# Forgetting attention in a two-layer trunk: values' products 12 steps later, V in two buffers, bias transfers on SyncE's queue, split last weight parts

## The chip, the cores and the metric

The kernel runs on one core of one Trainium2 chip. The core has five engines with an instruction stream each: TensorE (PE, matrix products into the accumulators of PSUM), VectorE (DVE), ScalarE (ACT), GpSimd (POOL) and SyncE (SP, which here only asks for transfers). The metric is the device time of one execution in microseconds, and lower is better.

## What is computed

Two decoder layers on one sequence of 256 tokens, model width 2048, in float32. Layer 0 mixes tokens with forgetting attention, 32 heads of 64; layer 1 with sliding-window attention. Cut to layer 0, which is all that the change touches:

```python
h = rmsnorm(x, norm_g[0])
p = h @ fox_w_in[0]                      # 2048 x 8224: q, k, v, gate, and 32 columns for log_f
q, k, v, gate = ...
log_f = log_sigmoid(p[..., 4*W:] + fox_b_f[0])
c = cumsum(log_f, axis=1)
s = (q @ k.T) * 64**-0.5 + c[t] - c[s]   # per head; masked where key > query
y = softmax(s) @ v
x = x + (y * silu(gate)) @ fox_w_out[0]
```

Layer 1 has the same frame with other attention, and a final RMSNorm ends the trunk.

## The kernel before, in words

**Products.** Each float32 product is made of split operands. A part of a weight matrix arrives as `wraw` by a DMA of SP's queue (`load`, L211, or L207 where one part is made of two blocks); ACT copies its leading bits into the "high" half of `w` (CAST, L224) and DVE subtracts to get the "low" half (L225). The activations lie in `xs` (layer input) or `ys` (attention output) as high and low too. Of a unit of weights (256 output columns, all 2048 inputs, four parts of four 128-row tiles), each tile gives two "wide" matmuls (512 columns: weight high by activation high and low) and two "narrow" ones (256 columns: weight low by activation high). The values' units run the other way round, activations as the stationary operand and three 512-column matmuls a tile. All matmuls have one line, L83, since a helper issues them; they are told apart by their tiles. There are five buffers for `w` and four for `wraw`, two accumulators `acc` for units and one more, `ps_s`, for scores; a third unit of the output projection borrows it.

**Stages of layer 0.** The 32 heads are eight groups of four (g = 0 to 7). A group has units q, k, gate, and values; the values of groups 1 and 2, 3 and 4, 5 and 6 come as one unit. Behind the last group comes the output projection (`out_units`), eight units whose results are added into `xT`. When a unit's last matmul is done, its consumer runs: for k, DVE adds the two halves (L613), scales (L614), ACT and DVE split the result in `kk` (L618, L619, L621, L622). For an output unit, ACT copies the upper half out (L319) and DVE adds twice (L736, L737), which sets the accumulator free for the unit three places on.

**Attention of a pair of heads.** It has stages, each on its own: the bias c[s] of the pair's keys is spread over 128 partitions by a DMA from `negc_d` into `bc` (L665, issued by POOL) and masked by POOL (L127); the scores of the second query block (`s`, PE from `kk` and `q` into `ps_s`, DVE L432 and L413); the scores of the first block some steps later (`s_first`); the softmax (ACT L361, DVE L369, L372); a transposition in two moves: DVE L453 into `staged`, a DMA to `turned_d` (L458) and four DMAs back into `pts` (L463), all issued by POOL; the values' products (PE `psy` from `pts` and `vg`), the gate (L547), and the split of the result into `ys` (L554).

**The order.** The matmuls stand in the program's order. The weight parts form one stream, and attention is hung into it: `tick` counts a step for every second matmul (every one and a half in the values' units), and a stage is registered to come so many steps after its group's k has been consumed. These numbers are tables, FOX_DUE for even groups, FOX_ODD, FOX_FIRST (group 0), FOX_NEXT (group 1) and FOX_LAST (group 7): for each of the two pairs of heads of a group the step of the first scores and the distance to the second ones, and then the step of the values' products. A bias is asked for 14 steps ahead of its scores (BIAS), or as many as the table's third number says. The other engines' order and SP's are set by a scheduler from dependencies and priorities: the consumers and the stages of attention have a raised one. Which transfers SP asks for and when follows from buffers: a weight part waits until the DVE instruction that read the buffer before it is done.

## Time and profile before

| what | us |
|---|---|
| three runs | 807.16, 811.65 (median), 812.43 |
| the profiled execution | 806.58 |
| span of its program | 804.8 |
| PE busy | 791.6 |
| DVE busy | 646.9 |
| ACT busy | 516.5 |
| POOL busy | 116.3 |

Of the span, layer 0's groups take about the first 403 us, its output projection what follows up to about 490 us. The granted TensorE clock was 0.997 of full speed. A row of the timeline reads: start, duration, engine, line, operation, output tile from input tiles, shapes, count, and in brackets how long the engine had been idle and what ended that. A row of the waits reads: engine, tile and line that waited, what it waited for, microseconds in all, times, the longest. "SPq" and "POOLq" are the queues of transfers that these engines ask for.

### The profile page before, as it was taken

How to read it: one execution, taken by the hardware profiler on the slowest of the kernel's cores; microseconds unless marked ns; L12 is line 12 of the kernel's file. 1: busy time of each engine (PE TensorE's matmuls, PEld its weight loads, DVE VectorE, ACT ScalarE, POOL GpSimd, SP SyncE). 2: the span in 40 equal slices, each digit the busy share in tenths (PEclk: the TensorE clock that was granted, in tenths of full speed). 3: DMA queues.
4: the chain of work that ended last, by engine and by line, in shares of the span. 5: the costliest groups of instructions: out<-in, count | busy, mean ns of one | idle time of the engine just before them, and what ended most of it. 6: DMA issues, size and time to landing. Idle time of an engine off the chain costs nothing.

```text
span 804.8 us, 13739 instructions
## 1 busy us (share of the span) xinstructions
PE 791.6 (98%) x4994; PEld 695.0 (86%) x4994; DVE 646.9 (80%) x1148; ACT 516.5 (64%) x947; POOL 116.3 (14%) x182
## 2 busy tenths in 40 slices
PE   8999999999999999999999999999999999999996
PEld 7988788888888888888888888888888888888885
DVE  6998986898688886888848768668999999977654
ACT  6876665665556565566537556567788786875651
POOL 1012340133202222021113110200000000001210
PEclk9999999999999999999999999999999999999998
DMA  8757797587866877577665655856445554455632
GB/s 276 253 195 267 243 302 214 177 269 234 249 186 202 257 252 240 189 214 247 195 218 170 210 188 161 223 155 209 153 158 189 185 180 152 155 192 188 198 122 105
DMA packets 52596, 164.43 MB, mean 204 GB/s; under 512 B 6977, under 2 KB 10209, under 8 KB 52529
## 3 DMA queue, kind: packets, MB, share of 16 engines
q1 hardware_dynamic: 44640, 141.84, 55.4%
q0 software_dynamic: 6736, 20.26, 9.0%
q10 hardware_dynamic: 1152, 1.47, 0.5%
q8 instruction: 39, 0.64, 0.3%
q14 instruction: 29, 0.23, 0.1%
HBM read 154.84 MB, written 8.70 MB: 203 GB/s over the span
## 4 chain that ended last, share of the span: by engine, by line
PE 84%; DVE 7%; DMA 4%; ACT 2%; issue 2%; SPq 0%; POOL 0%; DVEq 0%; ACTq 0%
PE acc L83 79%; DMA wraw<-in_fox_in_dram 3%; PE ps_s L83 2%; PE psy L83 2%; DVE w L225 2%; DMA pts<-turned_d 1%; ACT st L361 1%; DMA turned_d<-staged 1%; DVE st L372 1%; DVE staged L453 1%; DVE st L413 1%; DVE kk L622 1%; DVE kk L621 1%; PE psy_s L83 0%; ACT w L224 0%
## 5 line engine op out<-in xcount | busy, mean ns | idle before, releaser
L83 PE MATMUL acc<-xs,w 128*128 128x256 f32 (+1 forms) x2624 | 468.2, 337 | 0.3 <-ACT w L224 0.3
L83 PEld LDWEIGHTS acc<-xs,w 128*128 128x128 f32 x2624 | 404.6, 190 | 53.7 <-issue 0.7
L225 DVE TENSOR_TENSOR w<-wraw,w 128x1024 fp32r<-128x1024 f32 (+4 forms) x277 | 322.7, 1179 | 87.6 <-ACT w L224 86.6
L224 ACT CAST w<-wraw 128x1024 fp32r<-128x1024 f32 (+4 forms) x277 | 274.3, 1010 | 167.9 <-PE acc L83 122.1
L83 PE MATMUL acc<-ys,w 128*128 128x256 f32 (+1 forms) x960 | 168.3, 337 | 0.0
L83 PEld LDWEIGHTS acc<-ys,w 128*128 128x128 f32 x960 | 147.7, 190 | 19.4 <-issue 0.5
L83 PE MATMUL acc<-w,xs 128*128 128x512 f32 (+2 forms) x512 | 108.3, 361 | 1.1 <-ACT w L224 1.1
L83 PEld LDWEIGHTS acc<-w,xs 128*128 128x128 f32 x512 | 86.9, 188 | 16.1 <-ACT w L224 1.6
L361 ACT ACTIVATE st<-st,mx 128x256 f32<-128x256 f32 (+1 forms) x128 | 56.5, 443 | 12.6 <-DVE mx L413 8.1
L319 ACT COPY half<-acc 128x512 f32<-128x512 f32 x56 | 32.6, 583 | 33.1 <-PE acc L83 32.8
L463 POOL DMA_DIRECT2D pts<-turned_d x64 | 35.2, 556 | 55.5 <-DMA turned_d<-staged 40.2
L757 POOL TENSOR_TENSOR acc<-acc,sq 128x256 f32<-128x256 f32 x28 | 26.7, 954 | 82.5 <-ACT sq L751 81.4
L755 POOL COPY acc<-sq 128x256 f32<-128x256 f32 x2 | 1.3, 637 | 239.3 <-ACT sq L751 239.3
L83 PE MATMUL ps_s<-kk,q 128*128 128x256 f32 (+1 forms) x160 | 31.1, 307 | 2.0 <-DVE kk L622 1.4
L127 POOL TENSOR_SCALAR_AFFINE_SELECT bc<-bc 128x256 f32<-128x256 f32 x32 | 22.5, 720 | 70.4 <-DMA bc<-negc_d 70.4
L83 PEld LDWEIGHTS ps_s<-kk,q 128*128 128x128 f32 x160 | 24.8, 190 | 6.1 <-issue 3.0
L665 POOL DMA_DIRECT2D bc<-negc_d x16 | 9.0, 560 | 115.2 <-issue 101.6
L361 ACT ACTIVATION_READ_ACCUMULATOR st<-st,mx 128x1 f32 x128 | 24.0, 187 | 0.0
L380 ACT ACTIVATE st<-st,rl 128x128 f32<-128x128 f32 x64 | 23.9, 445 | 0.1
L159 DVE SCALAR_TENSOR_TENSOR xs<-xT,g_sb,xs 128x256 fp32r<-128x256 f32 x32 | 20.4, 667 | 3.5 <-ACT xs L158 3.5
L413 DVE CUSTOM_DVE_ANT_0 st<-ps_s,st 128x256 f32<-128x256 f32 (+1 forms) x64 | 20.3, 350 | 0.5
L158 ACT ACTIVATE xs<-xT,g_sb 128x256 fp32r<-128x256 f32 x32 | 15.5, 501 | 8.1 <-DVE xT L737 7.4
(144 smaller groups left out, 579.8 us busy)
## 6 DMA issues: line engine op xcount, KB each, us to landing
wraw<-in_fox_in_dram SPq DMA_DIRECT2D x96, 512.0 KB, 4.9
wraw<-in_swa_in_dram SPq DMA_DIRECT2D x72, 512.0 KB, 4.3
wraw<-in_fox_out_dram SPq DMA_DIRECT2D x32, 512.0 KB, 4.7
wraw<-in_swa_out_dram SPq DMA_DIRECT2D x32, 512.0 KB, 4.4
wraw<-in_fox_in_dram SPq DMA_DIRECT2D x54, 256.0 KB, 4.9
bc<-negc_d POOLq DMA_DIRECT2D x16, 384.0 KB, 5.2
turned_d<-staged POOLq DMA_DIRECT2D x16, 384.0 KB, 4.8
pts<-turned_d POOLq DMA_DIRECT2D x64, 96.0 KB, 5.3
```

The lines of the kernel that those rows point to most:

```text
L83: tc.keep_in_program_order(nc.tensor.matmul(*args, **kw))
L127: return nc.gpsimd.affine_select(out=ap, in_=ap, compare_op=ALU.is_ge, fill=NEG, base=base, pattern=pattern, channel_multiplier=mult,)
L158: nc.scalar.activation(xs[:, kt, 0, :], xT[:, kt, :], AF.Copy, scale=g)
L159: nc.vector.scalar_tensor_tensor(out=xs[:, kt, 1, :], in0=xT[:, kt, :], scalar=g, in1=xs[:, kt, 0, :].bitcast(F32), op0=ALU.mult, op1=ALU. ...
L224: state["split"] = nc.scalar.copy(high, raw)
L225: state["lows"] = [*state.get("lows", [])[-1:], nc.vector.tensor_tensor(out=low, in0=raw, in1=high.bitcast(F32), op=ALU.subtract)]
L319: nc.scalar.copy(s, ps[:, :, S : 2 * S])
L361: nc.scalar.activation(st[:, hh, rng], st[:, hh, rng], AF.Exp, scale=sign, bias=nm[:, qb, hh : hh + 1], accum_out=l[:, qb, hh : hh + 1],)
L380: nc.scalar.mul(st[:, hh, rng], st[:, hh, rng], rl[:, qb, hh : hh + 1])
L413: nc.vector.tensor_tensor_reduce(out=st, in0=high, in1=st if low is None else low, scale=self.scale, scalar=self.start(hh), op0=ALU.add, o ...
L463: nc.gpsimd.dma_start(out=pts[b * B : (b + 1) * B], in_=turned_d[b].rearrange("(a j) x -> j a x", j=B))
L757: nc.gpsimd.tensor_add(sums[0], sums[0], s)
```

## The change

- The values' products come 12 steps later in FOX_DUE and FOX_LAST, 15 in FOX_FIRST; those of FOX_NEXT and FOX_ODD keep their number.
- First scores move: the odd groups' from 22 to 27 and from 51 to 56, group 1's from 28 to 32 and from 59 to 64, the even groups' from 21 to 22 and from 52 to 50; group 1's second scores come 15 steps after the first instead of 12. Group 7's scores stay.
- The biases are asked for by SP instead of POOL, and 20 to 40 steps ahead of the scores instead of 14.
- `vg` (V) has two buffers instead of one. To make room, q and k share one tile, and a tile `r08` (the norm's scale times 1/8) is gone: q is scaled by one SCALAR_TENSOR_TENSOR instead of a TENSOR_TENSOR. Group 0's staging tiles are renamed to fit.
- The last of the four parts of the first three units of layer 0's output projection is two parts of two tiles each, and unit 0's last addition is put ahead of the two latest low subtractions on DVE.

```diff
--- before.py
+++ after.py
@@ -38,11 +38,11 @@
 SCALE_DUE = 8
 
 
-FOX_DUE = ((21, 12), (52, 13), 138)
-FOX_LAST = ((24, 12), (48, 13), 122)
-FOX_ODD = ((22, 12), (51, 12), 118)
-FOX_FIRST = ((57, 16, 32), (81, 12), 170)
-FOX_NEXT = ((28, 12), (59, 14), 120)
+FOX_DUE = ((22, 12, 20), (50, 13, 30), 150)
+FOX_LAST = ((24, 12, 20), (48, 13, 30), 134)
+FOX_ODD = ((27, 13, 25), (56, 13, 35), 118)
+FOX_FIRST = ((57, 16, 32), (81, 12, 40), 185)
+FOX_NEXT = ((32, 15, 25), (64, 14, 40), 120)
 SWA_DUE = ((36, 65), (53, 81), 91)
 SWA_LAST = ((36, 63), (51, 78), 86)
 
@@ -604,12 +604,14 @@
             with tc.high_priority(HP):
                 t = fox.tile([P, 2, S], F32, tag="q", name="q", bufs=1)
                 nc.vector.tensor_add(t, ps[:, :, 0:S], low_half(ps))
-                nc.vector.tensor_mul(t, t, each(state["r08"][:, 0:S]))
+                nc.vector.scalar_tensor_tensor(
+                    out=t, in0=t, scalar=SCALE, in1=each(r0()[:, 0:S]), op0=ALU.mult, op1=ALU.mult
+                )
                 self.qT = stack_q(t)
 
         def k(self, ps):
             with tc.high_priority(HP):
-                t = fox.tile([P, 2, S], F32, tag="k", name="k", bufs=1)
+                t = fox.tile([P, 2, S], F32, tag="q", name="k", bufs=1)
                 nc.vector.tensor_add(t, ps[:, :, 0:S], low_half(ps))
                 nc.vector.tensor_mul(t, t, each(r0()[:, 0:S]))
 
@@ -633,7 +635,7 @@
 
             def consume(c, ps):
                 if c == 0:
-                    self.vt = fox.tile([P, 2, 512], F32, tag="vg", name="vg", bufs=1)
+                    self.vt = fox.tile([P, 2, 512], F32, tag="vg", name="vg", bufs=2)
                     self.vg, other.vg = [None, None], [None, None]
                 nc.scalar.mul(self.vt[:, c, :], ps, r0()[:, S + c : S + c + 1])
                 self.vg[c], other.vg[c] = (self.vt[:, c, i * 256 : (i + 1) * 256] for i in range(2))
@@ -642,7 +644,7 @@
 
         def v(self, c, ps):
             if c == 0:
-                self.vt = fox.tile([P, 2, 512], F32, tag="vg", name="vg", bufs=1)
+                self.vt = fox.tile([P, 2, 512], F32, tag="vg", name="vg", bufs=2)
                 self.vg = [None, None]
             vg = self.vg[c] = self.vt[:, c, 0:256]
             if self.g > 0:
@@ -662,7 +664,7 @@
 
                 assert "forgot" in state
                 bc = fox.tile([P, 2, 3 * P], F32, tag="bc", name="bc")
-                nc.gpsimd.dma_start(out=bc, in_=negc_d[h0 : h0 + 2, :].partition_broadcast(P))
+                nc.sync.dma_start(out=bc, in_=negc_d[h0 : h0 + 2, :].partition_broadcast(P))
                 for hh in range(2):
                     diagonal = bc[:, hh, :].rearrange("p (b k) -> p b k", k=P)[:, 0:3:2, :]
                     filled = fill_where_not(diagonal, [[0, 2], [-1, P]], 0, 1)
@@ -705,10 +707,11 @@
             uq, uk = (
                 Unit(
                     cut(lambda a, b, w=fox_in_d[i, 0]: w[a // 8][:, a % 8 : a % 8 + b - a], QK_PARTS),
-                    "wgt", consume, stages=(half, (fox, own, 2 * S, 1), None, gt) + more, acc=acc,
+                    "wgt", consume, stages=(half, own, None, gt) + more, acc=acc,
                 )
                 for i, own, consume, more, acc in (
-                    (0, "q", G.q, (gt,), None), (1, "k", G.k, ((fox, "vg", 4 * S, 1),), (ps_s, "S")),
+                    (0, (fox, "q", 2 * S, 1), G.q, (gt,), None),
+                    (1, (fox, "pts_odd", 12 * P, 1), G.k, ((fox, "vg", 4 * S, 2),), (ps_s, "S")),
                 )
             )
             units += [uv, uq, uk, whole(fox_in_d[3, g], "wgt", gate_consumer(r0, G))]
@@ -734,16 +737,27 @@
             def consume(ps):
                 x = xT[:, 2 * u : 2 * u + 2, :]
                 nc.vector.tensor_add(x, low_half(ps), x)
-                nc.vector.tensor_add(x, ps[:, :, 0:S], x)
+                last = nc.vector.tensor_add(x, ps[:, :, 0:S], x)
+                if u == 0 and src is fox_out_d:
+                    ahead_of_lows(last)
                 for c in range(2):
                     done(2 * u + c)
 
             return consume
 
-        first = [
-            whole(src[u], "wgt", consumer(u), acts=ys, acc=(ps_s, "S") if u == 2 else None)
-            for u in range(3)
-        ]
+        def ends_late(u):
+            halves = [(src[u][1][:, k : k + 2, :], [2]) for k in (4, 6)]
+            return Unit(
+                quarters(src[u])[0:3] + halves, "wgt", consumer(u), acts=ys, acc=(ps_s, "S") if u == 2 else None
+            )
+
+        if src is fox_out_d:
+            first = [ends_late(u) for u in range(3)]
+        else:
+            first = [
+                whole(src[u], "wgt", consumer(u), acts=ys, acc=(ps_s, "S") if u == 2 else None)
+                for u in range(3)
+            ]
         return first + [whole(src[u], "wgt", consumer(u), acts=ys) for u in range(3, 8)]
 
     def square_into(sums, m):
@@ -1049,16 +1063,14 @@
         state["r0"] = r = inv_rms(
             [ssq0[:, 0, :]], "n0", ps_t.tile([P, 512], F32, tag="T", name="ps_n0")
         )
-        r08 = cpool.tile([P, S], F32, name="r08")
-        nc.vector.tensor_scalar_mul(r08, r[:, 0:S], SCALE)
-        state["r08"] = r08
 
     def in_turn(units):
         return [(u, p) for u in units for p in range(len(u.parts))]
 
     def out_stream(units):
 
-        early = [(u, p) for u in units[0:3] for p in range(3)] + [(u, 3) for u in units[0:3]]
+        late = len(units[0].parts) - 1
+        early = [(u, p) for u in units[0:3] for p in range(late)] + [(u, late) for u in units[0:3]]
         return early + in_turn(units[3:])
 
 
@@ -1123,7 +1135,9 @@
     def breaks(u, p):
 
         if u in turns:
-            return p in (1, 2) or p == 3 and u not in (first_out[0], last_out[0])
+            if u in first_out:
+                return p in (1, 3) or p == 4 and u is not first_out[1]
+            return p in (1, 2) or p == 3 and u is not last_out[0]
         return p % 2 == 1
 
     prev, held, wide_first = None, [], True
```

The number of matmuls and their sizes are the same. How instructions move is shown at three places.

PE, around the first pair's scores of group 5. Where `w` comes first in a row's inputs the matmuls are those of the values' unit of groups 5 and 6, `ps_s` are the scores (512 columns the first ones, 256 the second ones), `psy` the values' products of groups 3 and 4. Before, and with the change:

```order
L83 MATMUL acc<-xs,w 128x512 x14
L83 MATMUL acc<-xs,w 128x256 x32
L83 MATMUL acc<-xs,w 128x512 x16
L83 MATMUL acc<-w,xs 128x512 x33
L83 MATMUL ps_s<-kk,q_2702 128x512 x2
L83 MATMUL acc<-w,xs 128x512 x18
L83 MATMUL ps_s<-kk,q_2702 128x256 x2
L83 MATMUL acc<-w,xs 128x512 x12
L83 MATMUL psy<-pts,vg 64x256
```

```order
L83 MATMUL acc<-xs,w 128x512 x18
L83 MATMUL acc<-xs,w 128x256 x32
L83 MATMUL acc<-xs,w 128x512 x16
L83 MATMUL acc<-w,xs 128x512 x41
L83 MATMUL ps_s<-kk,q_2727 128x512 x2
L83 MATMUL acc<-w,xs 128x512 x19
L83 MATMUL ps_s<-kk,q_2727 128x256 x2
L83 MATMUL acc<-w,xs 128x512 x21
L83 MATMUL psy<-pts,vg 64x256
```

The first scores stand eight matmuls later, the second ones nine, and the values' products 18 later.

DVE, around the scaling of group 7's k (L614 before, L616 with the change). L453 writes `staged` of the pair before. Before, and with the change:

```order
L225 TENSOR_TENSOR w<-wraw,w 128x4x256
L453 STREAM_TRANSPOSE staged<-st 128x6x4x32
L613 TENSOR_TENSOR k<-acc,half 128x512
L225 TENSOR_TENSOR w<-wraw,w 128x4x256
L614 TENSOR_TENSOR k<-k,r_n_492 128x512
L621 TENSOR_TENSOR kk<-k,kk 64x2x256
L622 TENSOR_TENSOR kk<-k,kk 64x2x256
```

```order
L225 TENSOR_TENSOR w<-wraw,w 128x4x256
L453 STREAM_TRANSPOSE staged<-st 128x6x4x32
L225 TENSOR_TENSOR w<-wraw,w 128x4x256 x2
L615 TENSOR_TENSOR k<-acc,half 128x512
L616 TENSOR_TENSOR k<-k,r_n_492 128x512
L225 TENSOR_TENSOR w<-wraw,w 128x4x256
L623 TENSOR_TENSOR kk<-k,kk 64x2x256
```

The scaling of k now follows the addition at once; before, a low subtraction of a weight part (L225) stood between them. One more L225 stands ahead of the addition.

PE, at the end of the output projection's first three units. `acc` of the highest number here belongs to unit 3, which takes over the accumulator of unit 0, `acc_4064` before and `acc_4062` with the change. Before, and with the change:

```order
L83 MATMUL acc_4192<-ys_81,w_4155 128x512 x8
L83 MATMUL acc_4064<-ys_81,w_4168 128x512 x8
L83 MATMUL acc_4128<-ys_81,w_4189 128x512 x8
L83 MATMUL acc_4064<-ys_81,w_4168 128x256 x8
L83 MATMUL acc_4128<-ys_81,w_4189 128x256 x8
L83 MATMUL acc_4192<-ys_81,w_4231 128x256 x8
L83 MATMUL acc_4192<-ys_81,w_4231 128x512 x8
L83 MATMUL acc_4374<-ys_81,w_4244 128x512 x8
```

```order
L83 MATMUL acc_4216<-ys_81,w_4204 128x256 x4
L83 MATMUL acc_4216<-ys_81,w_4179 128x512 x8
L83 MATMUL acc_4216<-ys_81,w_4204 128x512 x4
L83 MATMUL acc_4062<-ys_81,w_4213 128x512 x4
L83 MATMUL acc_4062<-ys_81,w_4213 128x256 x4
L83 MATMUL acc_4139<-ys_81,w_4243 128x256 x4
L83 MATMUL acc_4216<-ys_81,w_4268 128x256 x4
L83 MATMUL acc_4139<-ys_81,w_4243 128x512 x4
L83 MATMUL acc_4216<-ys_81,w_4268 128x512 x4
L83 MATMUL acc_4387<-ys_81,w_4293 128x512 x8
```

Between unit 0's last matmul and unit 3's first one stood 24 matmuls (16 narrow ones and eight wide ones), and now stand 16 (eight of each). Ahead of these rows, between the last scores of group 7 and its values' products, stand 146 matmuls of this projection where 122 stood.

On SP's queue the 16 transfers into `bc` now stand between weight parts, among the last 32 parts of the input projection after the fifth, the ninth, the 24th and the 26th.

## The prediction

> **What bounds the kernel now.** I read the busy shares first, then the chain that ended last, the waits of PE, and PE's timeline where it waits.
>
> ```profile
> PE 791.6 (98%) x4994; PEld 695.0 (86%) x4994; DVE 646.9 (80%) x1148; ACT 516.5 (64%) x947; POOL 116.3 (14%) x182
> PE 84%; DVE 7%; DMA 4%; ACT 2%; issue 2%; SPq 0%; POOL 0%; DVEq 0%; ACTq 0%
> ```
>
> PE is busy 791.6 of 804.8 us, and the chain is PE's for 84%. The change takes no matmul away, so what can be won is PE's idle time, 13.2 us in all. Where it lies, the stretches tell (columns: length, then busy time of PE and its weight loads; DVE, ACT and POOL follow), with the waits of PE from 40 to 500 us:
>
> ```profile
> 45.00:110.00 65.00, 64.47 (x347) 54.67 (x346) 58.06 (x116) 41.15 (x75) 18.98 (x31) 1.00 0.74 243
> 190.00:290.00 100.00, 99.51 (x556) 85.74 (x552) 82.09 (x143) 60.18 (x98) 21.82 (x35) 1.00 0.74 226
> 290.00:390.00 100.00, 99.05 (x580) 86.87 (x579) 81.82 (x148) 62.21 (x101) 17.15 (x29) 1.00 0.68 213
> 390.00:420.00 30.00, 29.03 (x171) 25.09 (x170) 17.14 (x27) 13.43 (x21) 5.13 (x9) 1.00 0.79 239
> 790.00:804.80 14.80, 6.92 (x57) 6.55 (x55) 8.04 (x24) 2.01 (x6) 0.00 (x0) 0.82 0.39 142
> PE ps_s L83 <- DVE kk L622: 1.4, 2, 0.9
> PE psy L83 <- DMA pts<-turned_d: 1.0, 1, 1.0
> PE ps_s L83 <- DVE mx L413: 0.5, 1, 0.5
> ```
>
> The last stretch alone holds 7.9 us of the idle time, at the very end of the program, which the change doesn't touch. In the part that it does touch PE waits four times, 2.9 us together. Each has its row:
>
> ```profile
> 93.52 0.47 PE L83 MATMUL ps_s<-kk,q 128*128 128x256 f32 x2 [0.53 <-DVE mx L413]
> 275.22 0.47 PE L83 MATMUL ps_s<-kk,q 128*128 128x512 f32 x1 [0.49 <-DVE kk L622]
> 370.93 0.47 PE L83 MATMUL ps_s<-kk,q 128*128 128x512 f32 x1 [0.95 <-DVE kk L622]
> 412.68 0.88 PE L83 MATMUL psy<-pts,vg 128*64 128x256 f32 x8 [0.97 <-DMA pts<-turned_d]
> ```
>
> In this order: group 1's second scores, which want `ps_s` back from DVE; the first scores of group 5, then of group 7, which want `kk`; group 7's values, which want `pts` from its DMA. So the most that the change can win here, by this view, is 0.53 + 0.49 + 0.95 + 0.97 = 2.94 us, 0.36% of 806.58 us.
>
> **The change part by part.** A stage that comes later gains the matmuls now standing ahead of it. Their price:
>
> ```profile
> 269.81 4.70 PE L83 MATMUL acc<-w,xs 128*128 128x512 f32 x20
> 365.78 3.76 PE L83 MATMUL acc<-xs,w 128*128 128x256 f32 x30
> ```
>
> That is 4.70 / 20 = 0.235 us for a wide matmul and 3.76 / 30 = 0.125 for a narrow one.
>
> *Group 1, second scores:* 15 steps behind the first ones, not 12. In the values' unit a step is one and a half wide matmuls, so 3 x 1.5 x 0.235 = 1.06 us more cover against a wait of 0.53. It goes: -0.53. What follows on DVE (softmax, `staged`) is later by the same 1.06, but group 1's values keep their step 120 while its scores moved by 4 and 5; group 2, their mate, has its own later scores to wait for, and no row of PE shows a wait there.
>
> *Group 5, first scores:* eight wide matmuls later, 8 x 0.235 = 1.88 us against 0.49: -0.49.
>
> *Group 7, values:* between its last scores and its values stand eight wide and 16 narrow matmuls more, 8 x 0.235 + 16 x 0.125 = 3.88 us against 0.97: -0.97. The chain that sets it is the transposition's, and nothing in it is made longer:
>
> ```profile
> 397.32 0.98 DVE staged L453
> 398.59 5.74 DMA turned_d<-staged
> 404.61 1.64 POOL pts L463 x3
> 406.25 6.30 DMA pts<-turned_d
> ```
>
> The spread of its transfers says whether 3.88 - 0.97 = 2.9 us is margin enough: the landing of `pts` after its issue was 2.2 / 5.3 / 8.6 us (smallest, median, largest), so the 6.30 can grow by 2.3 to the largest seen and still be covered.
>
> ```profile
> DMA to landing us min/median/max: 2.2/5.3/8.6
> ```
>
> *Group 7, first scores:* their step stays 24, so no cover is added. Why they wait:
>
> ```profile
> 355.71 8.58 DMA wraw<-in_fox_in_dram
> 364.37 1.06 ACT L224 CAST w<-wraw 128x1024 fp32r<-128x1024 f32 x1 [1.59 <-DMA wraw<-in_fox_in_dram]
> 365.46 1.23 DVE L225 TENSOR_TENSOR w<-wraw,w 128x1024 fp32r<-128x1024 f32 x1 [0.44 <-ACT w L224]
> 366.61 0.69 DVE L614 TENSOR_TENSOR k<-k,r_n 128x512 f32<-128x512 f32 x1
> 367.32 0.62 ACT L618 CAST kk<-k 64x512 fp32r<-64x512 f32 x1 [1.90 <-DVE k L614]
> ```
>
> A weight part landed 8.58 us after its issue; ACT's CAST waited for it, DVE's low subtraction for the CAST, the scaling of k for the subtraction (in order on DVE), and `kk` for the scaling. With the change the scaling stands ahead of this subtraction. If the transfer lands as it did, the scaling ends when the addition before it does plus 0.69, and ACT can start `kk` when its CAST ends, 364.37 + 1.06 = 365.43 us or little later, and not at 367.32: about 1.5 us earlier, more than the wait. Against it, one more subtraction of 1.23 us stands ahead of the addition, and the bias's transfer now comes ahead of parts on one queue (below). So between -0.95 and, if 384 KB ahead of the part delay it by 384 / 276 = 1.4 us (276 GB/s moved in this stretch) and nothing of the 1.5 comes through, +1.4. I take -0.5, nearer the end that the new order speaks for.
>
> ```profile
> DMA packets 1337, 4.69 MB, mean 276 GB/s; under 512 B 197, under 2 KB 277, under 8 KB 1334
> ```
>
> *The halves.* The output projection's unit 3 starts 16 matmuls after unit 0's end, not 24: eight wide and eight narrow, 8 x 0.235 + 8 x 0.125 = 2.88 us, where 1.0 us more stood before. It needs unit 0's accumulator, free after this chain:
>
> ```profile
> 422.60 0.59 ACT L319 COPY half<-acc 128x512 f32<-128x512 f32 x1 [3.48 <-PE acc L83]
> 423.22 0.69 DVE L736 TENSOR_TENSOR xT<-half,xT 128x512 f32<-128x512 f32 x1 [2.84 <-ACT half L319]
> 424.02 0.69 DVE L737 TENSOR_TENSOR xT<-acc,xT 128x512 f32<-128x512 f32 x1
> ```
>
> From 422.60 to 424.71 that is 2.1 us. It fits in 2.88 with 0.8 left, if ACT and DVE are free as they were (idle 3.48 and 2.84 before); a CAST or subtraction begun just ahead costs up to 1.06 or 1.23. The second addition is put ahead of the low subtractions, so on DVE only one already running counts. Nothing to 1.23 - 0.8 = 0.4 for one engine, 1.5 for both: I take +0.3. In turn the last weights of unit 0 are loaded in smaller parts: three CASTs of half the length, three more DMA issues on SP, beside PE.
>
> *Biases on SP.* POOL is rid of 16 issues of 0.56 us, off the path (busy 14%). SP gets them, and there each stands ahead of weight parts:
>
> ```profile
> bc<-negc_d POOLq DMA_DIRECT2D x16, 384.0 KB, 5.2
> wraw<-in_fox_in_dram SPq DMA_DIRECT2D x96, 512.0 KB, 4.9
> ACT w L224 <- PE acc L83: 74.8, 40, 6.4
> ACT w L224 <- DMA wraw<-in_fox_in_dram: 8.0, 10, 1.6
> ```
>
> The same bytes move in the same stretches; only who goes first changes. From 45 to 420 us ACT's CASTs waited 74.8 us for PE to give a buffer back and 8.0 for a transfer, so parts mostly lie ready before they can be split, and PE waited for no weight between 40 and 500 us. A bias of 1.4 us ahead of a part goes into that cover: 0. If the cover were gone it would be 1.4 us for each of the 14 biases behind the first two, which come while group 0's attention is still far off. The first two wait on SP for the DMA that writes `negc_d`, and hold the weight parts behind them by about 1 us by their old issue times; the same cover hides it.
>
> [...]
>
> *Cover without price:* two buffers of `vg` take a wait away that PE's rows don't show; q and k in one tile add a wait of k's addition for q's last reader, which is done several microseconds before k's unit ends; the scaled q costs what it did, since an L339 of the same form takes as long as the multiplication at L607 (691 and 685 ns):
>
> ```profile
> L339 DVE SCALAR_TENSOR_TENSOR gate_e<-gt,gate_e 128x512 f32<-128x512 f32 x8 | 5.5, 691 | 3.3 <-ACT gate_e L338 3.3
> L607 DVE TENSOR_TENSOR q<-q,r 128x512 f32<-128x512 f32 x7 | 4.8, 685 | 0.1
> ```
>
> **Sum:** -0.53 - 0.49 - 0.97 - 0.5 + 0.3 = -2.2 us: 804.4 against the profiled execution's 806.58.
>
> **The rivals.**
>
> *Held weights (slower).* Each bias on SP waits for the tile of the pair two before it, and stands ahead of weight parts by 1.4 us of transfer. It decides where the delay is longer than a part has been lying ready. For it: 10 of 50 waits of CASTs are for DMA already. Against it: the mean wait for PE is 74.8 / 40 = 1.9 us, longer than 1.4. If half of the 14 come through to PE, 7 x 1.4 = 9.8 us: 806.9 (below) + 9.8 = 816.7; all of them, 826.5. Chance 0.11, of it 0.07 for slower than before by over 1%.
>
> *Deeper waits gone (faster).* The three runs lie at 807.16, 811.65 and 812.43, the profiled execution at 806.58. If the 5 us between are the same waits grown deeper with slower transfers, later stages take these away too: 806.58 - 2.94 = 803.6 for every run, and to 802 if waits that start to show are gone as well. For it: three of the four waits hang on or behind a transfer. Against it: no trace of a slower run is there. Chance 0.22, of it 0.13 for faster by over 1% (below 803.5).
>
> *Moved waits (no change).* Group 7's first scores wait as before or longer, and unit 3 waits up to 1.5 us for its accumulator: -1.99 + 1.4 + 1.5 = +0.9, 807.5 in the profiled execution's terms, in the runs' up to 812.5. For it: the margin of 0.8 is the thinnest in the new order. Chance 0.22.
>
> **How the numbers follow.** The forecast, -2.2 us in the profiled execution, has the remaining 0.45. The runs' median lies 811.65 - 806.58 = 5.1 us above that execution; I take half of this to stay, since some of it should be the deeper waits: 804.4 + 2.5 = 806.9, rounded to 807.0. The range goes from 802.0, the deeper waits gone, to 812.5, the moved waits on a run like the slowest shown. Taking 1% as about what a measurement of this kernel can tell from no change (803.5 to 819.8): faster 0.13, slower 0.07, within 0.80.
>
> **What would show it.** Right: PE's waits at group 1's second scores, group 5's first scores and group 7's values are gone from its list, the stretch from 390 to 420 us has 30.0 of PE busy and not 29.0, the wait of group 7's first scores is 0.5 or less, and no PE wait for `w` shows. Wrong: waits of CASTs for DMA well above 8.0 us with PE waiting for L224 or L225 (held weights); a PE wait of `acc` for L737's successor (the halves); the same times without the four waits would say that PE's own pace, and not its waits, is what differs between runs.

## The result, and the profile after

The changed kernel takes 803.92 us (median of six executions, 802.76 to 806.4), against 812.01 us for the kernel before (six, 807.16 to 812.5): ratio 0.9916, 95% interval 0.9888 to 0.9945 (the ratios and intervals are those on record, and differ a little from the quotients of the medians). A second comparison (experiment 5) gave 803.9 against 809.65 us, ratio 0.9934 (0.9908 to 0.9959). So it is faster by 0.7 to 0.8%, which is within 1%, though the first interval reaches past that. The forecast was 807.0 in a range from 802.0 to 812.5.

The page of the profiled execution after (802.76 us, span 801.0), first its busy times, then the shares of its chain:

```profile
PE 790.0 (99%) x4994; PEld 695.3 (87%) x4994; DVE 646.9 (81%) x1150; ACT 516.2 (64%) x950; POOL 104.8 (13%) x166
PE 94%; DVE 2%; DMA 2%; ACT 1%; issue 0%; SPq 0%; DVEq 0%; ACTq 0%
```

The chain was PE's for 84% and is for 94%: the detours over DVE and DMA are mostly gone (7% and 4% before, 2% each now). The stretches of the same lengths as before, up to 490 us, and all PE waits from 40 to 500 us:

```profile
45.00:110.00 65.00, 65.00 (x350) 56.09 (x349) 57.60 (x113) 40.90 (x69) 14.58 (x24) 1.00 0.76 240
190.00:290.00 100.00, 100.00 (x574) 86.57 (x574) 82.54 (x147) 59.19 (x98) 18.57 (x31) 1.00 0.74 232
290.00:390.00 100.00, 99.25 (x581) 87.17 (x580) 83.32 (x156) 63.61 (x108) 16.87 (x26) 1.00 0.69 213
390.00:420.00 30.00, 30.00 (x186) 26.52 (x185) 13.08 (x19) 12.04 (x19) 5.16 (x9) 1.00 0.68 208
420.00:490.00 70.00, 70.00 (x402) 61.87 (x401) 58.72 (x69) 43.34 (x71) 14.40 (x16) 1.00 0.63 203
PE ps_s L83 <- DVE kk L624: 0.8, 1, 0.8
```

Of the four waits three are gone; the 0.75 us left in the third stretch are group 7's first scores. Its chain, from the timeline (ACT, DVE and PE):

```profile
358.37 1.05 ACT L224 CAST w<-wraw 128x1024 fp32r<-128x1024 f32 x1 [3.24 <-DMA wraw<-in_fox_in_dram]
360.42 1.05 ACT L224 CAST w<-wraw 128x1024 fp32r<-128x1024 f32 x1 [1.01 <-DMA wraw<-in_fox_in_dram]
361.50 1.23 DVE L225 TENSOR_TENSOR w<-wraw,w 128x1024 fp32r<-128x1024 f32 x1 [0.83 <-ACT w L224]
362.64 0.68 DVE L615 TENSOR_TENSOR k<-acc,half 128x512 f32<-128x512 f32 x1
363.36 0.69 DVE L616 TENSOR_TENSOR k<-k,r_n 128x512 f32<-128x512 f32 x1
368.05 0.47 PE L83 MATMUL ps_s<-kk,q 128*128 128x512 f32 x1 [0.75 <-DVE kk L624]
```

The scaling (L616) now follows the addition (L615) at once, as the order said. But the weight parts before it landed late (3.24 and 1.01 us of waiting on ACT), and the low subtraction that now stands ahead of the addition waits for them, so `kk` is again ready too late for the scores, by 0.75 us.

Against the profiled execution before, PE's idle time fell by 2.2 us (13.2 to 11.0) and its busy time by 1.6 us, 3.8 us of span. Matmul ends are modelled, so part of a wait can be counted as busy time; the 1.6 us are not assigned further here. The medians moved by more, 8.1 us in the first comparison and 5.8 in the second. That is what the experiments had to explain.

### The profile page after: what moved, and what is told of

It reads as the page before. It is cut to its first block, busy times and chain, and to the rows that moved or that the text cites. A ratio compares the mean times of both kernels' runs of the same rounds, so it can differ in the third digit from the quotient of the medians.

```text
span 801.0 us, 13775 instructions
## 1 busy us (share of the span) xinstructions
PE 790.0 (99%) x4994; PEld 695.3 (87%) x4994; DVE 646.9 (81%) x1150; ACT 516.2 (64%) x950; POOL 104.8 (13%) x166
## 4 chain that ended last, share of the span: by engine, by line
PE 94%; DVE 2%; DMA 2%; ACT 1%; issue 0%; SPq 0%; DVEq 0%; ACTq 0%
PE acc L83 88%; PE ps_s L83 3%; PE psy L83 2%; DMA wraw<-in_fox_in_dram 1%; DMA wraw<-in_vf_dram 1%; DVE w L225 1%; PE psy_s L83 0%; ACT st L361 0%; ACT w L224 0%; DVE scaled L866 0%; DVE kk L623 0%; SPq L211 0%; ACT q L390 0%; DVE st L413 0%; DVE st L372 0%
## 5 line engine op out<-in xcount | busy, mean ns | idle before, releaser
L225 DVE TENSOR_TENSOR w<-wraw,w 128x1024 fp32r<-128x1024 f32 (+4 forms) x280 | 323.0, 1170 | 85.4 <-ACT w L224 84.3
L224 ACT CAST w<-wraw 128x1024 fp32r<-128x1024 f32 (+4 forms) x280 | 274.7, 1000 | 168.8 <-PE acc L83 113.3
L127 POOL TENSOR_SCALAR_AFFINE_SELECT bc<-bc 128x256 f32<-128x256 f32 x32 | 20.0, 647 | 169.9 <-DMA bc<-negc_d 109.5
L413 DVE CUSTOM_DVE_ANT_0 st<-ps_s,st 128x256 f32<-128x256 f32 (+1 forms) x64 | 20.2, 350 | 0.5
L509 DVE STREAM_TRANSPOSE turned<-st 128x768 f32<-128x768 f32 x16 | 15.6, 975 | 4.2 <-ACT st L380 4.0
```

Of the source, the lines that this page charges most:

```text
L127: return nc.gpsimd.affine_select(out=ap, in_=ap, compare_op=ALU.is_ge, fill=NEG, base=base, pattern=pattern, channel_multiplier=mult,)
L224: state["split"] = nc.scalar.copy(high, raw)
L225: state["lows"] = [*state.get("lows", [])[-1:], nc.vector.tensor_tensor(out=low, in0=raw, in1=high.bitcast(F32), op=ALU.subtract)]
L413: nc.vector.tensor_tensor_reduce(out=st, in0=high, in1=st if low is None else low, scale=self.scale, scalar=self.start(hh), op0=ALU.add, o ...
L509: nc.vector.transpose(turned.rearrange("p h k -> p (h k)"), self.st.rearrange("p h k -> p (h k)"))
```

## The experiments

Each is compared with the kernel before, measured beside it on the same chip: 1 to 4 together, 5 to 8 together, and 9 to 12 together. The waits named are PE's between 40 and 500 us in the one profiled execution of each.

**1. The values' steps of before.**

```diff
-FOX_DUE = ((22, 12, 20), (50, 13, 30), 150)
+FOX_DUE = ((22, 12, 20), (50, 13, 30), 138)
...
-FOX_LAST = ((24, 12, 20), (48, 13, 30), 134)
+FOX_LAST = ((24, 12, 20), (48, 13, 30), 122)
...
-FOX_FIRST = ((57, 16, 32), (81, 12, 40), 185)
+FOX_FIRST = ((57, 16, 32), (81, 12, 40), 170)
```

> The changed kernel with the values' steps of before (138, 122, 170), all else as changed. Theory (each stage gains only the wait that its own place had): PE waits about 1.0 us for the transfer of pts again at group 7's values, and a little more in slower executions: 805 to 807 us, ratio to before 0.992 to 0.995. Rival (the values' waits are what grows in the runs at 812 us): 809 to 812 us, ratio 0.997 to 1.000.

805.07 us (803.54 to 808.9), ratio 0.9959 (0.9938 to 0.9979). The time is as expected (the ratio a little above), the place is not: it is group 0's values that wait for `pts`, not group 7's, and no trace of before shows a wait there. The transfers into `pts` of that group's second pair landed up to 10.0 us after they were asked for, against 3.9 to 4.8 before.

```profile
108.33 0.88 PE L83 MATMUL psy<-pts,vg 128*64 128x256 f32 x8 [1.41 <-DMA pts<-turned_d]
369.98 0.47 PE L83 MATMUL ps_s<-kk,q 128*128 128x512 f32 x1 [0.95 <-DVE kk L624]
```

**2. The biases by GpSimd, at the change's steps.**

```diff
-                nc.sync.dma_start(out=bc, in_=negc_d[h0 : h0 + 2, :].partition_broadcast(P))
+                nc.gpsimd.dma_start(out=bc, in_=negc_d[h0 : h0 + 2, :].partition_broadcast(P))
```

> The changed kernel with the biases asked for by GpSimd again, as early as in the change. Theory (the queue of the biases is off the path): 803 to 805 us, ratio 0.990 to 0.993, no new wait of PE. Rival A (biases on SyncE's queue hold weights): faster than the change, 801 to 803 us, and group 7's first scores wait less than 0.75 us. Rival B (on GpSimd's queue the biases stand behind the transposition's transfers and come late): 806 us or more, with a wait of PE for DVE's L413, L432 or L444 behind a late bias.

803.18 us (802.4 to 804.11), ratio 0.9928 (0.9906 to 0.995): as fast as the change. Group 7's first scores do not wait here, group 1's second ones do (0.91 us, for L413), so a bit of each rival shows in one profile, and neither in the time. The queue of the biases is worth nothing that can be measured.

**3. Whole last parts, no addition put ahead.**

```diff
-        if src is fox_out_d:
-            first = [ends_late(u) for u in range(3)]
-        else:
-            first = [
...
+        first = [
+            whole(src[u], "wgt", consumer(u), acts=ys, acc=(ps_s, "S") if u == 2 else None)
+            for u in range(3)
+        ]
```

(unit 0's last addition and the order of these parts' matmuls as before, too).

> The changed kernel with the output projection's first three units in four parts again, and without the addition put ahead of the low subtractions. Theory (the halves matter for the hand-over to unit 3 alone, and that is not waited for): 803 to 805 us, ratio 0.990 to 0.993, no new wait. Rival (the halves keep 24 matmuls, 12 x 0.235 + 12 x 0.125 = 4.3 us, ahead of the first product that needs group 7's output, and the later values need them): a PE wait of acc for L554's ys appears, 0 to 1 us in the profile and more in slow runs, 804 to 808 us.

805.12 us (804.34 to 806.32), ratio 0.9944 (0.992 to 0.9967). The rival's wait is there: the output projection waits for group 7's output.

```profile
415.95 63.75 PE L83 MATMUL acc<-ys,w 128*128 128x512 f32 x366 [0.57 <-DVE ys L554]
```

That is what the halves do; in the time it can't be told from the changed kernel's 0.9934, since the intervals overlap. A whole last part has products with tiles 12 to 15; the half holds tiles 14 and 15 alone back, which are group 7's.

**4. The scores' steps of before.**

```diff
-FOX_DUE = ((22, 12, 20), (50, 13, 30), 150)
+FOX_DUE = ((21, 12, 19), (52, 13, 32), 150)
...
-FOX_ODD = ((27, 13, 25), (56, 13, 35), 118)
+FOX_ODD = ((22, 12, 20), (51, 12, 30), 118)
...
-FOX_NEXT = ((32, 15, 25), (64, 14, 40), 120)
+FOX_NEXT = ((28, 12, 21), (59, 14, 35), 120)
```

> The changed kernel with the steps of the first and second scores of before (21 and 52, 22 and 51, 28 and 59; 12 steps from first to second in group 1), the biases asked for at the same steps as in the change. Theory (each place its own wait): 0.5 us at group 1's second scores and 0.5 us at an odd group's first scores come back, 804 to 806 us, ratio 0.992 to 0.994. Rival (these waits are the ones that grow in the runs at 812 us): 807 to 810 us, ratio 0.995 to 0.998, with waits at the first scores of several odd groups.

807.42 us (806.05 to 810.38), ratio 0.9981 (0.9964 to 0.9999): the rival's size. The waits, in the order of time:

```profile
94.36 0.47 PE L83 MATMUL ps_s<-kk,q 128*128 128x256 f32 x2 [1.20 <-DVE mx L413]
181.57 0.47 PE L83 MATMUL ps_s<-kk,q 128*128 128x512 f32 x1 [0.30 <-DVE kk L624]
276.24 0.47 PE L83 MATMUL ps_s<-kk,q 128*128 128x512 f32 x1 [0.30 <-DVE kk L624]
277.66 0.47 PE L83 MATMUL ps_s<-kk,q 128*128 128x512 f32 x1 [0.95 <-ACT w L224]
```

The wait of group 1 is 1.20 us and not 0.53. DVE's rows say why: `staged` of the pair before (L453, 0.97 us) now lies between the two reductions that set `ps_s` free.

```profile
92.58 0.41 DVE L413 CUSTOM_DVE_ANT_0 st<-ps_s,st 128x256 f32<-128x256 f32 x1
92.92 0.97 DVE L453 STREAM_TRANSPOSE staged<-st 128x768 f32<-128x768 f32 x1
93.82 0.38 DVE L413 CUSTOM_DVE_ANT_0 st<-ps_s,st 128x256 f32<-128x256 f32 x1
```

In before L453 ran at 94.55, behind both. Group 7's wait, on the other hand, is not there. A likely reason is that PE comes later and the weights have landed (ACT's casts waited less than 6.4 us for them from 45 to 420 us, 15.2 in the changed kernel).

**5. The changed kernel again.** No edit.

> The changed kernel itself, to stand beside the other runs of this call. Theory (its gain is what the four waits take, more in slower executions of before): ratio to before 0.990 to 0.994. Rival (part of the first comparison's 8 us was the chip's): 0.994 to 0.998.

803.9 us (802.61 to 806.32), ratio 0.9934 (0.9908 to 0.9959). The only wait is 0.95 us at group 7's first scores.

**6. The scores' steps alone, in the kernel before.**

```diff
-FOX_DUE = ((21, 12), (52, 13), 138)
+FOX_DUE = ((22, 12), (50, 13), 138)
...
-FOX_ODD = ((22, 12), (51, 12), 118)
+FOX_ODD = ((27, 13), (56, 13), 118)
...
-FOX_NEXT = ((28, 12), (59, 14), 120)
+FOX_NEXT = ((32, 15), (64, 14), 120)
```

> The kernel before with the change's steps of first and second scores alone; values, one V buffer, biases on GpSimd 14 steps ahead and whole last parts as before. Theory (the scores' steps are the larger part, since the change without them kept 0.2% of its 0.8%): ratio 0.994 to 0.997; the waits of group 1 and group 5 are gone, those of group 7's first scores (about 1 us) and values (1 us or more) stay. Rival (the gains do not add, since a wait removed early is taken up by the next one that hangs on the same transfers): ratio 0.998 to 1.000, with the waits at group 7 or at a values' product grown to 2 us or more.

810.46 us (807.04 to 814.95), ratio 1.0017 (0.9991 to 1.0044): the rival. The profiled execution took 813.78 us. The waits of groups 1 and 5 are gone, and the values' products of groups 0 and 7 wait:

```profile
111.49 1.25 PE L83 MATMUL psy<-pts,vg 128*64 128x256 f32 x8 [3.99 <-DMA pts<-turned_d]
373.76 0.47 PE L83 MATMUL ps_s<-kk,q 128*128 128x512 f32 x1 [0.20 <-DVE kk L622]
417.47 0.88 PE L83 MATMUL psy<-pts,vg 128*64 128x256 f32 x8 [2.93 <-DMA pts<-turned_d]
```

Group 0's wait is new. PE reaches its values at 106.62 us, 1.2 us earlier than before (107.86): the 0.53 us of waiting for group 1's scores are gone, and the last of these scores, ahead of the values before (106.33), stand behind them now (112.67). The rest, some 2.8 us, lies in the transfers: GpSimd asks for those of the second pair into `pts` from 102.22 us on in both executions, and the one that PE waits for lands 7.54 us after its request here (103.86 to 111.40), while the four took 3.9 to 4.8 before. Why they are slower is not shown. Group 7's wait is not new: before has 2.96 us there in experiment 9. And there is a second price, in the granted clock (the third number from the right) of the stretches around the two waits:

```profile
105.00:111.50 6.50, 2.51 (x23) 2.00 (x21) 2.80 (x6) 1.05 (x1) 1.53 (x4) 1.00 1.00 279
111.50:114.00 2.50, 2.50 (x14) 2.02 (x15) 0.50 (x2) 1.23 (x2) 0.97 (x2) 0.57 0.68 267
114.00:118.00 4.00, 4.00 (x25) 3.74 (x25) 3.29 (x11) 3.38 (x11) 1.78 (x4) 0.84 0.65 201
417.40:420.00 2.60, 2.53 (x19) 2.32 (x20) 0.69 (x1) 0.94 (x1) 0.00 (x0) 0.82 0.23 52
420.00:424.00 4.00, 4.00 (x19) 3.66 (x19) 2.96 (x3) 1.67 (x3) 0.00 (x0) 0.69 0.42 147
```

After the first wait the clock was 0.57 for 2.5 us and 0.84 for 4.0, and the eight products behind it took 1.25 us where the eight ahead of it had taken 0.88. If PE's work goes with the granted clock, the price is an estimate from these rows: 2.5 x 0.43 + 4.0 x 0.16 = 1.7 us lost after the first wait, and 2.6 x 0.18 + 4.0 x 0.31 = 1.7 us again after the second. By it the waits of 3.99 and 2.93 us here cost about half as much once more.

**7. Group 7's first scores later, in the changed kernel.**

```diff
-FOX_LAST = ((24, 12, 20), (48, 13, 30), 134)
+FOX_LAST = ((28, 12, 24), (50, 13, 32), 134)
```

> The changed kernel with group 7's first scores four steps later for its first pair and two for its second (28 and 50), 8 wide matmuls or 1.9 us more cover. Theory (the last wait is that of kk behind late weights, 0.75 us in the profile and more in slower executions): no PE wait is left between 40 and 480 us, 1 to 2 us faster than the changed kernel in this call. Rival (the wait only moves on, to group 7's values or its output, whose cover shrinks by the two steps): the same time within 0.5 us and a new wait of psy or acc.

802.77 us (801.75 to 804.16), ratio 0.9918 (0.9888 to 0.9949). Group 7's wait is gone and none took its place near it; one of 0.29 us showed at group 5's first scores. The median is 1.1 us below the changed kernel's (5), as the theory had it, but the intervals of the two ratios overlap. It is the fastest kernel of the study by its median, on one comparison.

**8. One buffer of V, in the changed kernel.**

```diff
-                    self.vt = fox.tile([P, 2, 512], F32, tag="vg", name="vg", bufs=2)
+                    self.vt = fox.tile([P, 2, 512], F32, tag="vg", name="vg", bufs=1)
...
-                self.vt = fox.tile([P, 2, 512], F32, tag="vg", name="vg", bufs=2)
+                self.vt = fox.tile([P, 2, 512], F32, tag="vg", name="vg", bufs=1)
```

(the staging tile of the same name too).

> The changed kernel with one buffer of V instead of two. Theory (with the values later, V of the next groups is ready before the values of the ones before have been read: in the order of the change 3 matmuls or 0.7 us and the scores lie between the values' products of groups 3 and 4 and the rest of the unit that writes V): PE waits for nothing, but ACT writes V later and the transfer chain is not touched, same time within 1 us. Rival (the accumulators of V's unit are held until the buffer is free, and PE waits for them): a PE wait of acc for L638 or L645 of 0.5 us or more, twice.

805.15 us (803.27 to 808.31), ratio 0.9941 (0.9917 to 0.9965), 1.25 us above the changed kernel's median (5), with overlapping intervals. Beside the known wait of group 7's first scores PE waits once, for V to be written:

```profile
116.17 29.50 PE L83 MATMUL acc<-xs,w 128*128 128x512 f32 x172 [1.03 <-ACT vg L640]
```

The rival's mechanism is there, once and not twice: group 0's later values keep the only V buffer while the V of groups 1 and 2 is ready, and the accumulator of their unit is held.

**9. The kernel before again.** No edit.

> The kernel before itself, to see its longer executions: its runs so far lay between 805.6 and 814.7 us. Theory (the four waits, those that hang on the transposition's transfers above all, grow to 3 us or more in the longer executions, and the granted clock of PE drops after such a wait as in the run with the scores' steps alone): ratio 1.000; if its profile is of an execution at 810 us or more, it shows a wait of 3 us or more and a granted clock below 0.95 in the stretch after it. Rival (PE's own pace differs, its waits do not): the waits are the same 2.9 us in a profile at 810 us or more.

809.83 us (803.63 to 814.4), ratio 0.9987 (0.9952 to 1.0022). The profiled execution took 809.36 us. Its waits, and the stretches around the last one:

```profile
92.75 0.48 PE L83 MATMUL ps_s<-kk,q 128*128 128x256 f32 x2 [0.49 <-DVE mx L413]
179.92 0.47 PE L83 MATMUL ps_s<-kk,q 128*128 128x512 f32 x1 [0.34 <-DVE kk L622]
275.42 0.47 PE L83 MATMUL ps_s<-kk,q 128*128 128x512 f32 x1 [0.94 <-DVE kk L622]
413.60 0.88 PE L83 MATMUL psy<-pts,vg 128*64 128x256 f32 x8 [2.96 <-DMA pts<-turned_d]
```

```profile
413.60:416.00 2.40, 2.40 (x18) 2.15 (x19) 0.69 (x1) 0.82 (x1) 0.00 (x0) 0.82 0.15 31
416.00:420.00 4.00, 4.00 (x19) 3.71 (x19) 2.96 (x3) 1.79 (x3) 0.00 (x0) 0.68 0.45 163
420.00:424.00 4.00, 4.00 (x19) 3.30 (x18) 1.23 (x1) 1.05 (x1) 0.00 (x0) 1.00 0.57 162
```

In the 806.58 us execution that the prediction was made from, group 7's first scores waited 0.95 us and its values 0.97. Here the scores don't wait, the values wait 2.96, and by the same estimate the lower clock behind them loses 2.4 x 0.18 + 4.0 x 0.32 = 1.7 us. The size of this wait is that of the two moves of the transposition. Their transfers in this execution, in 12 and in 6:

```profile
397.53 6.42 DMA turned_d<-staged
405.86 7.59 DMA pts<-turned_d
401.51 6.21 DMA turned_d<-staged
409.64 6.98 DMA pts<-turned_d
401.43 6.03 DMA turned_d<-staged
409.38 7.95 DMA pts<-turned_d
```

Together they took 14.01, 13.19 and 13.98 us, and group 7's values waited 2.96, 2.12 and 2.93; in the execution that the prediction was made from they took 12.04, and the wait was 0.97. Each time the wait is the sum less 11.05 to 11.07, whatever the scores' steps and the biases' queue.

Of the 34 executions of before measured beside 9 to 12, the 18 above 811 us had a mean granted clock of 0.994, the ten below 809 us one of 0.997. The profile does not reach the 810 us that the expectation named, and of the four waits only this one grew to some 3 us; its place and the clock behind it are the theory's.

**10. The values' steps alone, with two V buffers and the tiles that make room, in the kernel before.**

```diff
-FOX_DUE = ((21, 12), (52, 13), 138)
-FOX_LAST = ((24, 12), (48, 13), 122)
+FOX_DUE = ((21, 12), (52, 13), 150)
+FOX_LAST = ((24, 12), (48, 13), 134)
...
-FOX_FIRST = ((57, 16, 32), (81, 12), 170)
+FOX_FIRST = ((57, 16, 32), (81, 12), 185)
```

> The kernel before with the change's steps of the values (150, 134, 185), two buffers of V and the tiles that make room; scores, biases and last parts as before. Theory (the wait of group 7's values goes, and in longer executions that of group 0's; the waits of the scores stay and show): 806 to 808 us, ratio 0.995 to 0.998. Rival (the values are what made the longer executions long, so their later steps alone give the gain): 803 to 805 us, ratio 0.991 to 0.994.

808.11 us (806.57 to 810.58), ratio 0.9975 (0.9952 to 0.9999): the theory. Its waits are those of the scores, at groups 1, 3 and 5, and one that the theory did not name, for group 7's output (as in 3):

```profile
94.02 0.48 PE L83 MATMUL ps_s<-kk,q 128*128 128x256 f32 x2 [1.30 <-DVE mx L413]
181.50 0.47 PE L83 MATMUL ps_s<-kk,q 128*128 128x512 f32 x1 [0.56 <-DVE kk L624]
277.38 0.47 PE L83 MATMUL ps_s<-kk,q 128*128 128x512 f32 x1 [0.95 <-DVE kk L624]
418.80 63.75 PE L83 MATMUL acc<-ys,w 128*128 128x512 f32 x366 [0.57 <-DVE ys L554]
```

**11. Scores' and values' steps together, with the V buffers; biases by GpSimd 14 steps ahead, whole last parts.** The tables' edits of 6 and 10 in one kernel.

> The kernel before with the change's steps of scores and values, two buffers of V and the tiles that make room; biases by GpSimd 14 steps ahead and whole last parts as before. Theory (the two tables' moves need each other, and the rest of the change gives little): ratio 0.993 to 0.995, no wait of psy for pts of 0.5 us or more, a wait of acc for ys of 0 to 1 us since the last parts are whole. Rival (the biases' earlier asking is needed too): ratio 0.997 or more, with waits for L413 or L432 behind a bias.

803.77 us (803.02 to 804.84), ratio 0.9929 (0.9905 to 0.9954): the theory. One wait is left, 0.57 us for group 7's output. So the two tables' moves, with the V buffers, give as much as the whole change, as far as the intervals tell.

**12. The biases alone, in the kernel before.**

```diff
-FOX_DUE = ((21, 12), (52, 13), 138)
+FOX_DUE = ((21, 12, 19), (52, 13, 32), 138)
...
-                nc.gpsimd.dma_start(out=bc, in_=negc_d[h0 : h0 + 2, :].partition_broadcast(P))
+                nc.sync.dma_start(out=bc, in_=negc_d[h0 : h0 + 2, :].partition_broadcast(P))
```

(the other tables' thirds likewise).

> The kernel before with the biases asked for by SyncE and at the change's steps; all else as before. Theory (the bias's queue matters to the transposition alone, whose transfers GpSimd issues too): 0 to 2 us faster than before, ratio 0.997 to 1.001, with the waits of group 1, 5 and 7 still there. Rival (the biases hold the weights behind them): slower than before, ratio 1.002 or more, with casts that wait for DMA well above 8 us and PE waits for L224.

809.75 us (806.1 to 813.03), ratio 0.9992 (0.9963 to 1.0021). The waits of groups 1, 5 and 7 are all there, with one at group 3, 5.9 us in its profiled execution. No gain in the time, and ACT's casts waited 10.2 us for weights, little more than the 8.0 before.

## Why the prediction was right, and where it was not

The time fell inside the range, the direction and "within 1%" held. It came out 3.1 us below the forecast, near the 803.6 us of the rival "deeper waits gone" and 0.4 us above the 803.5 where "faster by over 1%" began, so that "within 1%" held narrowly, and partly by luck. Point by point, by its own steps.

*The bound.* That the idle time of PE in layer 0 was what could be won is borne out: the kernels with less than 1 us of waiting left (the changed one, 2, 7, 11) lie at 802.8 to 803.9 us, those with 1.4 to 2.4 us (1, 3, 8) at 805.1 to 805.2, those with 2.7 us and more (4, 6, 9, 10, 12) at 807.4 to 810.5.

*Group 1, group 5, group 7's values (-0.53, -0.49, -0.97).* All three waits are gone, as the matmuls counted had it, and with the old scores' steps (4) those of groups 1 and 5 are back. At group 5 the margin is thin: 0.29 us came back in the profile of 7, and at group 1's second pair 0.91 in that of 2. Group 7's values wait in four of the five profiles with their old step (not in 1) and in none of the nine with the new one.

*Group 7's first scores (-0.5).* Mis-sized: 0.95 us became 0.75 in one profiled execution and 0.95 in the other. The moved scaling did what the order said, and the extra subtraction ahead of the addition took it back, because the parts it waits for landed late. In all, ACT's casts waited 15.2 us for weights where they waited 8.0 before. That is half of what the prediction named as the sign of held weights; the other half, PE waiting for L224 or L225, is not there. The biases' queue does not make this sum: with the biases on GpSimd it is 14.7 (2) and 15.1 us (11). It goes with how little PE waits: 12.8 to 20.4 us in the eight profiles with less than 2.5 us of PE waiting (the changed kernel's two, 1, 2, 3, 7, 8, 11), at most 13.1 in those with 2.7 and more (before's two, 4, 6, 10, 12). That a PE that pauses less uses weights earlier is my reading of it, not shown. At this one place, though, the queue may matter. With the step kept, group 7's first scores wait 0.75 us or more in six of the seven profiles with biases on SyncE's queue (not in 4), and 0.20 us or nothing in 2, 6, 10 and 11, with biases on GpSimd; but also 0.95 in one of before's two. That would be the prediction's own rival, held weights, in small. The times don't show it.

```profile
ACT w L224 <- PE acc L83: 66.4, 37, 4.0
ACT w L224 <- DMA wraw<-in_fox_in_dram: 15.2, 8, 3.2
```

*The halves (+0.3).* Wrong by a missed purpose. Unit 3 does not wait (the stretch from 420 to 490 us is 70.00 busy). What I did not cost is that the halves keep products with group 7's output back; without them 0.57 us of waiting for `ys` comes wherever the values are late (3, 10, 11).

*V's two buffers (0).* The zero was right as a change against before, the reason was not: the second buffer removes no wait of before, it prevents one of 1.03 us that the later values would make (8).

*Biases on SP (0).* Right for the time, by 2 and 12. How soon a bias landed hardly differed between the two queues either: in the kernel before a bias landed 5.2 us (median) after its issue on GpSimd's queue and 5.3 on SyncE's (12), in the changed kernel 5.8 on GpSimd's (2) and 5.7 on SyncE's. The rows of 12, of 2 and of the changed kernel:

```profile
bc<-negc_d SPq DMA_DIRECT2D x16, 384.0 KB, 5.3
bc<-negc_d POOLq DMA_DIRECT2D x16, 384.0 KB, 5.8
bc<-negc_d SPq DMA_DIRECT2D x16, 384.0 KB, 5.7
```

*The sum and the base.* The step that failed is "I take half of this to stay": that half of the 5.1 us between the profiled execution and the median would remain. With the change 803.92 - 802.76 = 1.2 us of it remained (and in 5 the profiled execution, 804.25 us, lies above the median of 803.9). As far as the traces reach, longer executions of before are waits grown, as the rival "deeper waits gone" had it with 803.6 us: from 806.58 to 809.36 us the waits grew by 1.8 us, and the clock behind the longest cost 1.7 by the estimate of 9, together a little more than the 2.8 us between the two. That clock is a part of the price that the prediction did not have at all. The trace of before ends at 809.36 us; what makes an execution of 812 us is inferred from the granted clocks alone.

*Sums of independent terms.* The sum took each wait by itself. They do not add: the scores' steps alone gain nothing (6), the values' alone 0.25% (10), both together 0.7% (11). What they make for each other stands in the rows. The scores' steps make group 0's values wait (3.99 us in 6, 1.41 in 1), and the values' later step takes that away. The values' steps alone leave group 1's scores waiting 1.30 us and not 0.53 (10), as in 4: `staged` (L453) comes to lie between the two reductions on DVE, and this wait ends at 94 us, ahead of any values' product, so it is not PE's arrival that makes it. The other waits in 10 (groups 3 and 5) are no longer than in 12. Which of the scores' moves matters most was not tried one by one.

Left open is what makes the transfers into `turned_d` and `pts` of group 7 take 5.74 and 6.30 us in one execution of before and 6.42 and 7.59 in another, and those into `pts` of group 0 up to 4.8 us there and up to 10.0 in 1; the runs show that they vary, not why.

## What to carry to other kernels

In a stream of work that one engine bounds, a wait that is removed moves the engine forward, and a later consumer of a slow transfer can come to wait, as group 0's values did for 3.99 us in 6, where PE came 1.2 us earlier: moves along such a chain have to be judged together, and a part that is worth nothing alone can give more than half of the gain beside another (6, 10, 11). Where runs spread while the profile shows waits on transfers, ask what those waits are in the longer executions before taking the spread for noise. And a part of a change that seems to have no price or gain may be there to keep another part from making a new wait (the second V buffer one of 1.03 us, 8, the halves one of 0.57, 3).

## What the runs showed of the hardware

A PE wait of 2.93 to 3.99 us (by modelled matmul ends) was followed by a granted clock of 0.57 to 0.84 for some 6.5 us, about 1.7 us lost each time by the estimate of 6, three times in two kernels (twice in 6, once in 9). Shorter waits did not show it: behind the 0.97 us wait in the profiled execution before (its rows below) and behind the longest of experiment 12 (2.12 us, the last two rows) the clock stayed 1.00. In the 4.00 us that begin 2.2 to 2.6 us after the wait of group 7's values, the traces of these two have 24 matmuls each, and those of 6 and 9 have 19 each, at a clock of 0.69 and 0.68.

```profile
412.60:415.00 2.40, 2.32 (x20) 2.11 (x21) 0.69 (x1) 0.73 (x1) 0.00 (x0) 1.00 0.44 151
415.00:419.00 4.00, 4.00 (x24) 3.47 (x23) 2.96 (x3) 2.72 (x4) 0.00 (x0) 1.00 0.43 161
416.75:419.00 2.25, 2.25 (x20) 2.00 (x21) 0.69 (x1) 0.67 (x1) 0.00 (x0) 1.00 0.12 26
419.00:423.00 4.00, 4.00 (x24) 3.49 (x23) 2.96 (x3) 2.72 (x4) 0.00 (x0) 1.00 0.44 156
```

That the wait brings the lower clock is read from their order in time in these three places; how long a wait it takes was not tried.
